# The last 2 KB of a load by another DMA queue, which leaves one DMA engine out

## The chip, the cores and the metric

The kernel runs on one core of a Trainium2 chip. The metric is device time in microseconds, from the start of the program on the chip to its end; the median of several runs counts. All engines of the core (TensorE, VectorE, ScalarE, GpSimd, SyncE) run programs of their own and meet through semaphores. Data moves between HBM and the on-chip memory (SBUF) by 16 DMA engines, which all queues share.

## The reference

```python
def setup_inputs():
    batch, heads, seq, dim = 8, 8, 512, 64
    return {"q": randn(batch, heads, seq, dim).astype(np.float32),
            "k": randn(batch, heads, seq, dim).astype(np.float32)}

def reference(q, k):
    scale = 1.0 / np.sqrt(q.shape[-1])
    return (np.einsum('bhqd,bhkd->bhqk', q, k) * scale).astype(np.float32)
```

For each of 64 pairs of batch and head, a 512 x 64 matrix of queries is multiplied with a 512 x 64 matrix of keys, and the 512 x 512 scores are scaled by 1/8. The inputs are 8.4 MB each, the output is 67.1 MB, all in float32.

## The kernel before

The batch is cut into four units (`UNITS`) of two batches each. A unit has four groups of work (two batches, and two halves of the heads), so there are 16 groups (`ALL`), of which each makes 2 x 8 matmuls and fills a quarter of the tile `big`. This tile holds 128 partitions x 4 parts x 32 KB. It is used twice: first the loads of unit `v` land in part `v` (`xf(v)`, 16 KB of k and 16 KB of q in each partition), later the scores are gathered there for the stores.

**Loads.** The first k load is cut in two halves, one issued by SyncE and one by ScalarE (line 72). The seven others are issued by SyncE in the order q0, k1, q1, k2, q2, k3, q3, each with a semaphore of its own (lines 81 to 84). A load fills 128 partitions with one contiguous run of 16 KB from HBM each, 2 MB in all. SyncE issues all of them without any wait, and the DMA engines work through them in that order.

**Casts.** GpSimd waits for each load and casts it to bfloat16 in two halves (lines 113 to 136), into a layout that lets VectorE turn pairs of values at once. There are slots for three units (`SLOTS`), so the casts of the last unit wait until VectorE has turned unit 0 (`turned`, line 115). The last two casts are those of q of the last unit; they wait for `load_sems[7]`.

**Turning.** VectorE turns keys and queries by 32 x 32 transposes (lines 191 to 238) into `kT` and `qz`.

**Matmuls and evacuation.** TensorE multiplies in a loop of four rounds of four groups (lines 141 to 164). ScalarE (and VectorE for six pieces) scales the sums from PSUM into `big` (lines 170 to 186), 2048 values per partition at a time.

**Stores.** SyncE stores `big` to HBM as soon as the groups are there (lines 93 to 107): two stores of 4 MB and seven of 8 MB. When a store has landed, its semaphore (`free0`, `free1`) lets TensorE begin the groups that will fill that part again, so two stores are under way in turn. At the end SyncE waits until the last two have landed (line 109). Loads and stores of SyncE share one DMA queue, so that on each DMA engine the stores stand behind the loads.

Of the kernel before, what the change touches and what calls it, by code (L numbers as in the profile page):

```python
# [5 lines left out]
def kernel(  # L6
# [5 lines left out]
    nc = tc.nc  # L12
    B, H, S, D = q.shape
    scale = 1.0 / (D ** 0.5)
    P = 128
    Q = 32
    UNITS = B // 2
# [4 lines left out]
    RO = 8  # L22
# [2 lines left out]
    ALL = 2 * B  # L25
    SETS = 2 * UNITS
    SLOTS = UNITS - 1

    f32 = mybir.dt.float32
    bf16 = mybir.dt.bfloat16  # L30
# [6 lines left out]
    sem = {name: nc.alloc_semaphore(name) for name in names}  # L37
    load_sems = [nc.alloc_semaphore(f"load{n}") for n in range(2 * UNITS)]
    halves = [load_sems[0], nc.alloc_semaphore("load0b")]

    q_r = q.rearrange("(v b) (x s h) (m j) d -> v (s h m) (b x) (j d)", b=2, x=2, s=2, j=R)
# [7 lines left out]
    bigs = [big[:, n] for n in range(UNITS)]  # L52
    xb = nc.alloc_sbuf_tensor("xb", [P, 2 * SLOTS, J, D, 2], bf16)[:]
    kT = nc.alloc_sbuf_tensor("kT", [P, 2 * G, S], bf16)[:]
# [2 lines left out]

    xw = xb.rearrange("p n w d e -> p n (w d e)").bitcast(f32).rearrange(
        "p n (w d) -> p n w d", d=D)
    kw = kT.bitcast(f32)  # L60
    qw = qz.bitcast(f32)

    def xf(v):
        return bigs[v].rearrange("p x i k -> p (x i k)").rearrange("p (x s c) -> p x s c", x=2, s=2)

    def slot(v, x):
        return v % SLOTS * 2 + x

    for s, queue in enumerate((nc.sync, nc.scalar)):
        first_load = queue.dma_start(
            out=xf(0)[:, 0, s].rearrange("p (x c) -> p x c", x=2), in_=k_0[s]
# [4 lines left out]

    for n in range(1, 2 * UNITS):
        v, x = divmod(n, 2)
        nc.sync.dma_start(out=xf(v)[:, x].rearrange("p s c -> p (s c)"), in_=(k_r, q_r)[x][v]
                          ).then_inc(load_sems[n], 16)

    def store(to, tiles):
# [22 lines left out]

    for v in range(UNITS):
        if v == SLOTS:
            nc.gpsimd.wait_ge(sem["turned"], 1)
            nc.gpsimd.sem_inc(sem["free1"], 1)
        for x in range(2):
            if v or x:
                nc.gpsimd.wait_ge(load_sems[2 * v + x], 16)
            for s in range(2):  # L120
                if v == x == 0:
                    nc.gpsimd.wait_ge(halves[s], 16)
                src = xf(v)[:, x, s]
                dst = xb[:, slot(v, x)]
                if x == 0:
                    src = src.rearrange("p (w e d) -> p w e d", e=2, d=D)
                    dst = dst[:, s * J // 2:(s + 1) * J // 2].rearrange("p w d e -> p w e d")
                else:
                    src = src.rearrange("p (jj e i d) -> p jj e i d", e=2, i=RO, d=D)
                    dst = dst.rearrange("p (i jj) d e -> p jj e i d", i=RO)[  # L130
                        :, s * JJ // 2:(s + 1) * JJ // 2]
                cast = nc.gpsimd.tensor_copy(out=dst, in_=src)  # L132
            cast.then_inc(sem["ready"], 1)
        if v % 2 == 0:
            nc.gpsimd.wait_ge(sem["ready"], 2 * v + 2)
            nc.gpsimd.sem_inc(sem[f"free{v // 2}"], 32)
# [132 lines left out]
```

## Time and profile before

| | |
|---|---|
| Time, median of 3 runs | 200.11 us (200.09 to 200.56) |
| Span of the profiled execution | 199.1 us |
| Moved by DMA | 83.90 MB, mean 421 GB/s |
| HBM read, written | 16.78 MB, 67.11 MB |
| Casts on GpSimd | 16, 2470 ns each |
| Evacuations on ScalarE | 58, 1888 ns each |
| Loads: issue to landing | 11.5 / 24.2 / 37.1 us (least, median, most) |
| First store issued, last store issued | 35.8 us, 175.9 us |

The page gives for each engine the time in which it was busy, its share of the span, and how many instructions it ran. One row shows the DMA engines in 40 slices of the span, as the mean busy share of all 16 in tenths, 9 for 90% or more. The DMA queues have rows of their own: packets, megabytes, and the time that the packets took as a share of 16 engines' span. A row of a timeline gives the start and the length of an instruction in us, its engine, line and tiles, and in brackets how long the engine had been idle and what ended that. For a queue (SPq) the length is that of the issuing, or from the first to the last of several. A row of waits gives the sum in us, the number of waits and the longest. Beside these views the trace holds a record for each DMA packet (start, length, queue, bytes; not the engine) and the time of each addition that a DMA engine makes to a semaphore.

### The profile page before, as it was taken

The page shows a single profiled execution, that of the slowest core. Times are in us where ns is not written, and L with a number is a line of the kernel's source. Part 1 is how long each engine was busy: PE and PEld are TensorE (multiplying, and loading weights), DVE is VectorE, ACT ScalarE, POOL GpSimd, SP SyncE. Part 2 cuts the span into 40 slices and gives each one's busy share as a digit, 9 for nine tenths or more (in the row PEclk, how much of TensorE's full clock was granted, in tenths as well). Part 3 has the DMA queues.
Part 4 walks back from the last instruction along what each step waited for, and adds up shares of the span by engine and source line. Part 5 has one row for each costly group of instructions (what it writes and reads, how often), then busy time and mean ns, then how long its engine had stood idle before and what let it go on. Part 6 is the DMA issues. An engine that isn't in the chain of part 4 may idle for free.

```text
span 199.1 us, 729 instructions
## 1 busy us (share of the span) xinstructions
PE 79.9 (40%) x256; PEld 23.5 (12%) x256; DVE 113.8 (57%) x61; ACT 105.6 (53%) x59; POOL 38.9 (20%) x20
## 2 busy tenths in 40 slices
PE   0000356546624662565257516550766076600000
PEld 0000011111101110111021102110211021100000
DVE  4238999999478039944993599369926500400000
ACT  2000049949970977197629752974397449730000
POOL 0399999699000000000000000000000000000000
PEclk9999999979995899589957975998599859995555
DMA  6999999999999999999999999999999999999995
GB/s 199 449 431 428 425 421 425 431 438 441 434 428 421 421 421 421 474 441 434 428 428 421 421 430 434 456 434 441 428 428 428 421 421 434 448 441 448 428 428 224
DMA packets 3746, 83.90 MB, mean 421 GB/s; under 512 B 288, under 2 KB 288, under 8 KB 800
## 3 DMA queue, kind: packets, MB, share of 16 engines
q1 hardware_dynamic: 3472, 82.84, 97.2%
q10 hardware_dynamic: 272, 1.05, 1.3%
q14 instruction: 2, 0.02, 0.0%
HBM read 16.78 MB, written 67.11 MB: 421 GB/s over the span
## 4 chain that ended last, share of the span: by engine, by line
DMA 41%; ACT 32%; PE 6%; DVE 4%; POOL 2%; issue 0%; SPq 0%
DMA out_dram<-big 35%; ACT big L179 32%; PE ps L158 6%; DMA big<-in_q_dram 6%; DVE qz L205 4%; POOL xb L132 2%; SPq L89 0%; SPq L107 0%
## 5 line engine op out<-in xcount | busy, mean ns | idle before, releaser
L179 ACT ACTIVATE big<-ps 128x2048 f32<-128x2048 f32 x58 | 104.3, 1888 | 68.3 <-PE ps L158 68.3
L158 PE MATMUL ps<-kT,qz 128*128 128x512 bf16 x256 | 79.9, 450 | 94.0 <-DMA out_dram<-big 35.8
L205 DVE STREAM_TRANSPOSE qz<-xb 32x1024 f32<-32x1024 f32 (+1 forms) x36 | 65.2, 1810 | 1.3 <-POOL xb L132 0.7
L158 PEld LDWEIGHTS ps<-kT,qz 128*128 128x128 bf16 x256 | 23.5, 110 | 149.8 <-ACT big L179 48.7
L132 POOL CAST xb<-big 128x2048 bf16<-128x2048 f32 x16 | 38.7, 2470 | 10.3 <-DMA big<-in_k_dram 7.8
L177 DVE TENSOR_SCALAR big<-ps 128x2048 f32<-128x2048 f32 x6 | 13.8, 2292 | 43.2 <-PE ps L158 43.2
L200 DVE STREAM_TRANSPOSE kT<-xb 64x1024 f32<-64x1024 f32 (+1 forms) x18 | 31.4, 1747 | 11.5 <-POOL xb L132 6.8
L212 DVE MEMSET qz<- 128x4096 uint32 x1 | 3.5, 3472 | 2.9 <-PEq L77 2.9
L179 ACT ACT_TABLE_LOAD x1 | 1.3, 1283 | 2.0 <-PEq L77 2.0
L253 POOL MEMSET const-float32-0.0<- 128x1 f32 x1 | 0.1, 98 | 0.2 <-issue 0.2
L253 POOL MEMSET const-bfloat16-1.0<- 128x1 bf16 x1 | 0.1, 101 | 0.0
L253 POOL MEMSET const-uint8-127<- 128x1 uint8 x1 | 0.1, 101 | 0.0
L253 POOL MEMSET const-float32-1.0<- 128x1 f32 x1 | 0.1, 98 | 0.0
## 6 DMA issues: line engine op xcount, KB each, us to landing
out_dram<-big SPq DMA_DIRECT2D x7, 8192.0 KB
big<-in_q_dram SPq DMA_DIRECT2D x4, 2048.0 KB, 24.2
out_dram<-big SPq DMA_DIRECT2D x2, 4096.0 KB
big<-in_k_dram SPq DMA_DIRECT2D x3, 2048.0 KB, 24.2
big<-in_k_dram ACTq DMA_DIRECT2D x1, 1024.0 KB, 9.0
big<-in_k_dram SPq DMA_DIRECT2D x1, 1024.0 KB, 7.5
```

Source lines behind the costliest of these rows:

```text
L132: cast = nc.gpsimd.tensor_copy(out=dst, in_=src)
L158: ins = pe.matmul(out=ps[:, i], lhsT=qz[:, 2 * t + x, i], rhs=kT[:, 2 * t + x], start=True, stop=True)
L177: freed = nc.vector.tensor_scalar_mul(out=to, in0=src, scalar1=scale)
L179: freed = nc.scalar.mul(out=to, in_=src, mul=scale)
L200: return nc.vector.transpose(out=out, in_=src)
L205: return nc.vector.transpose(out=qw[d:d + Q, b % 2 * G:(b % 2 + 1) * G, rows, h * Q:(h + 1) * Q].rearrange("d g i (m jj) -> d i jj m g", j ...
L212: nc.vector.memset(qz, 0.0).then_inc(sem["zeroed"], 1)
L253: nc = _bacc.Bacc("TRN2", target_bir_lowering=False, num_devices=1)
```

## The change

The last load, q of unit 3, is cut. Of the 16 KB in each partition the first 14 KB (`CUT` = 3584 values) come as before from SyncE, in one transfer of 128 partitions. The last 2 KB come in another way:

- for the first 120 partitions (`MOST`) by one transfer that GpSimd issues on its software queue, before its first cast;
- for the last 8 partitions by two transfers of 4 partitions each, which SyncE issues behind the large one.

Ahead of its transfer GpSimd resets the cursor of its queue and moves 5 x 2 runs of 32 bytes into a small tile `step` that nobody reads[...]. The purpose is that the 120 partitions go to 15 DMA engines, 8 each, without number 4, and the 8 others to the engines 0 to 3. Engine 4 so carries 16 KB less, and engines 0 to 3 carry 4 KB more each. The total of the bytes stays, but for the 320 bytes of `step`.

Before the last two casts GpSimd now waits for both of its transfers (`rest`, 32) and for the three of SyncE (48 on the last load's semaphore).

```diff
+    CUT = RO * S - 512
+    MOST = 120
...
+    rest_sem = nc.alloc_semaphore("rest")
...
+    step = nc.alloc_sbuf_tensor("step", [5, 2, 8], f32)[:]
...
-    for n in range(1, 2 * UNITS):
+    last_q = xf(UNITS - 1)[:, 1].rearrange("p s c -> p (s c)")
+    for n in range(1, 2 * UNITS - 1):
         v, x = divmod(n, 2)
         nc.sync.dma_start(out=xf(v)[:, x].rearrange("p s c -> p (s c)"), in_=(k_r, q_r)[x][v]
                           ).then_inc(load_sems[n], 16)
+    nc.sync.dma_start(out=last_q[:, :CUT], in_=q_r[UNITS - 1, :, :, :CUT]).then_inc(load_sems[-1], 16)
+    for n in range(MOST // 4, P // 4):
+        nc.sync.dma_start(out=last_q[4 * n:4 * n + 4, CUT:], in_=q_r[UNITS - 1, n, :, CUT:]
+                          ).then_inc(load_sems[-1], 16)
...
+    nc.gpsimd.inc_swdge_sem([], [], mode="reset_dge_cursor")
+    nc.gpsimd.dma_start(out=step, in_=q_r[0, 0:5, 0:2, 0:8]).then_inc(rest_sem, 16)
+    nc.gpsimd.dma_start(out=last_q[:MOST, CUT:], in_=q_r[UNITS - 1, :MOST // 4, :, CUT:]
+                        ).then_inc(rest_sem, 16)
...
-            if v or x:
+            if 2 * v + x == 2 * UNITS - 1:
+                nc.gpsimd.wait_ge(rest_sem, 32)
+                nc.gpsimd.wait_ge(load_sems[-1], 48)
+            elif v or x:
                 nc.gpsimd.wait_ge(load_sems[2 * v + x], 16)
```

## The prediction

> **What bounds the kernel now.** I read the page from its DMA rows down, because a kernel that moves 83.9 MB in 199 us is suspect there first.
>
> ```profile
> span 199.1 us, 729 instructions
> PE 79.9 (40%) x256; PEld 23.5 (12%) x256; DVE 113.8 (57%) x61; ACT 105.6 (53%) x59; POOL 38.9 (20%) x20
> DMA  6999999999999999999999999999999999999995
> q1 hardware_dynamic: 3472, 82.84, 97.2%
> q10 hardware_dynamic: 272, 1.05, 1.3%
> q14 instruction: 2, 0.02, 0.0%
> ```
>
> No compute engine passes 57%, while the 16 DMA engines are at 90% or more in every slice but the first and the last. Queue 1 alone takes 97.2% of sixteen engines' span. So the time is the bytes of the busiest DMA engine over its rate. The chain of waits shows "DMA out_dram<-big" pieces of 23.4 us; they are pieces of a queue that never runs empty, as the sync queue's timeline and its waits show:
>
> ```profile
> 5.96 0.62 SPq L83 DMA_DIRECT2D big<-in_q_dram  x1
> 35.77 23.55 SPq L89 DMA_DIRECT2D out_dram<-big  x3
> 97.73 0.61 SPq L89 DMA_DIRECT2D out_dram<-big  x1
> 175.90 0.61 SPq L89 DMA_DIRECT2D out_dram<-big  x1
> ...
> SPq L109 <- DMA out_dram<-big: 22.6, 1, 22.6
> ```
>
> All loads are issued by 6.6 us and land by 43.08 us, the first store stands ready from 35.77 us, and the last, issued at 175.90, lands 23 us later although its 8 MB take only about 19.4 us: it queues. In the packet records nearly every 32 KB store packet takes 1213 to 1214 ns, one per 1210.5 ns on an engine. That is 27 GB/s each, without a gap.
>
> The tail is the point here. The page's last DMA digit, 5, covers 5 us, and the windows view shows in which part of it traffic is thin:
>
> ```profile
> 197.00:199.12 2.12, 0.00 (x0) 0.00 (x0) 0.00 (x0) 0.00 (x0) 0.00 (x0) 0.50 0.04 15
> ```
>
> Packets count where they start, so hardly anything starts after 197.00. Each DMA engine adds one to a store's semaphore when its share has landed. Those times, from the trace, in us:
>
> ```
> store   1st     8th     15th    last    last - 8th
>  1    52.18   52.30   52.65   52.82   0.52
>  3    81.26   81.37   81.86   82.01   0.63
>  5   119.99  120.14  120.81  121.09   0.95
>  7   158.75  158.98  159.53  160.17   1.19
>  9   197.52  197.75  198.25  199.07   1.33
> ```
>
> The last arrival falls behind steadily, and at the end it is 0.83 us behind the fifteenth. The packet records show why: among the store packets is a row of packets of 1220 to 1236 ns that follow each other at 1221 to 1224 ns. That is one engine, about 11 ns slower per packet; times 128 packets this is 1.4 us. One slow engine therefore sets the end, and the other fifteen wait up to 1.5 us for it. The trace doesn't record its number.
>
> [...]
>
> **The change part by part.** First, cost per row. A 4 KB row follows the next at 155.5 ns and a 16 KB row at 607.5 ns, so one KB costs 37.7 ns and each row about 5 ns besides.
>
> Engine 4 has 8 rows of the last q load. They shrink by 2 KB each: 8 x 2 x 37.7 = 0.60 us saved. A second reading agrees: load landings lie 4.89 us apart for 128 KB per engine, so 16 KB are 0.61 us. It gains two 32-byte rows of the step transfer (8-byte to 32-byte packets of the instruction queue took 7 ns) and at most two semaphore posts (9 ns): 0.03 to 0.05 us. Net 0.56 us less on engine 4.
>
> Engines 5 to 15 move the same bytes in 8 rows more: 8 x 5 ns, and posts: 0.06 to 0.07 us more. Engines 0 to 3 get two rows of 2 KB (80 ns each) on top and two posts: 0.25 us more in all.
>
> If engine 4 is the slow one, its end moves from 199.07 to 198.51 us. The fifteenth, at 198.25, moves to 198.32, or to 198.50 if it is one of 0 to 3. Either way the new end is about 198.51, 0.56 us sooner. The whole kernel is nowhere else shortened.
>
> What lies beside other work: SyncE issues two instructions more (0.6 us each, from 6.6 to 7.8 us), ahead of a store that isn't ready before 35.77. The waits added at the last q cast (rest and 48 of the load) stand on GpSimd. Queued behind them are only the two last casts, and VectorE's turning of the last q behind those. The trace puts them late enough:
>
> ```profile
> 8.28 4.81 POOL L132 CAST xb<-big 128x2048 bf16<-128x2048 f32 x2 [7.83 <-DMA big<-in_k_dram]
> 39.81 9.67 POOL L132 CAST xb<-big 128x2048 bf16<-128x2048 f32 x4 [1.87 <-DVE qz L205]
> ...
> 2.89 3.47 DVE L212 MEMSET qz<- 128x4096 uint32 x1 [2.89 <-PEq L77]
> ```
>
> The last q casts begin at about 44.6 us, and the load landed at 43.08. So these waits cost nothing.
>
> GpSimd's two transfers stand ahead of the first cast. GpSimd idles until 8.28 us, so up to about 6 us of issuing are free. No row of before prices such an issue. From below: 0.6 us each, as on sync. [...]
>
> Their 16 KB per engine also come ahead of the first loads and delay them by 0.6 us. This moves the first casts from 8.28 to about 8.9, and through casts, transposes and evacuations the third store from 58.65 to about 59.3. That store is needed when the first two have drained, at 61.9 on the first engines, less 1.1 us from issue to first packet: slack is 61.9 - 1.1 - 58.65 = 2.1 us. Of that 0.6 is used. No bubble, no cost.
>
> Sum: 200.11 - 0.56 = 199.55 us.
>
> **The rivals.** First, slower: the late engine isn't number 4. Then its work grows by 0.07 us, or 0.25 us on engines 0 to 3: 200.18 to 200.36 us. For it speaks that the trace gives no number; against it, nothing in the profile. Second, slower by more: GpSimd's descriptors come so late that the slack of 2.1 us is spent. With a first cast 3 to 4 us late [...] and the 0.6 us for bytes, 1.5 to 2.5 us of empty queue appear on all engines: 200.11 + 1.5 to 2.5 - 0.56, so 201.05 to 202.05 us. Against it: GpSimd has nothing else to do before 8.28 us. Third, a smaller gain: rows written by the software queue cost more than 5 ns, say 60, so that fifteen engines lose 0.5 us, and another becomes the last, at 198.75 or 198.9: 199.8 to 199.95 us. For it: before has no queue of this kind; against it: 4 KB rows in two alternating queues cost no extra time.
>
> **How the numbers follow.** Forecast 0.58; late engine another one 0.13; large slowdown 0.16; other engines become last 0.13. The forecast's own spread is 0.2 us around 199.55, since the drift of 1.4 us need not be the same in each run; it lies almost on the bound of 0.3% (199.51), so I give six tenths of it, 0.36, to faster (the reading by landings, 0.61, passes the bound), and the rest, with the third rival and most of the first, to no change: faster 0.36, same 0.45, slower 0.19. From 199.35 to 200.40 the range holds the forecast, the first and the third rival, leaving out the large slowdown and a little on the fast side.
>
> **What would show it.** A software queue with some 120 packets of 2 KB on the page; the last landing of the ninth store within 0.3 us of the fifteenth instead of 0.83; its end near 198.5. If the gap stays at 0.8 or grows, the wrong engine was relieved. If a zero or a low DMA digit appears near 60 us, or the first cast starts after 10.5 us, the second rival is right. If the fifteenth moved by 0.5 us, the third. The forecast is wrong altogether if the slow engine is slow only while it is being recorded, for then timed runs have nothing to relieve.

## The result, and the profile after

The changed kernel is slower: 200.87 us (median of 8 runs, 200.41 to 201.20) against 200.11, a ratio of 1.0032 with a 95% interval of 1.0020 to 1.0045. The prediction was 199.55, range 199.35 to 200.40.

The page of the changed kernel, its span, two rows of slices and its DMA queues:

```profile
span 199.5 us, 731 instructions
...
DMA  6999999999999999999999999999999999999997
GB/s 205 389 395 427 424 427 443 415 449 427 420 453 466 420 440 420 420 420 420 427 427 466 460 422 420 420 416 427 434 420 434 447 440 440 427 427 427 420 427 309
...
q1 hardware_dynamic: 3488, 82.59, 97.2%
q10 hardware_dynamic: 272, 1.05, 1.4%
q0 software_dynamic: 112, 0.25, 0.4%
```

Read the two rows together. The engines are as busy as before from the second slice on, and the last digit went from 5 to 7: the tail is fuller, as it was meant to be. But the second and third slice move 389 and 395 GB/s. The same row of the kernel before, which the prediction didn't show:

```profile
GB/s 199 449 431 428 425 421 425 431 438 441 434 428 421 421 421 421 474 441 434 428 428 421 421 430 434 456 434 441 428 428 428 421 421 434 448 441 448 428 428 224
```

So the DMA engines are busy and slow, early on. The windows view (columns: us, busy time and instructions of PE, PEld, DVE, ACT, POOL, clock, DMA share, GB/s) narrows it to a stretch of 4.3 us, first the kernel before, then after:

```profile
8.00:12.30 4.30, 0.00 (x0) 0.00 (x0) 0.00 (x0) 0.00 (x0) 4.02 (x2) 1.00 1.00 430
```

```profile
8.00:12.30 4.30, 0.00 (x0) 0.00 (x0) 0.00 (x0) 0.00 (x0) 3.65 (x2) 1.00 1.03 347
```

430 minus 347 GB/s for 4.3 us is 0.36 MB, or 0.83 us at 430 GB/s. The packet records say what is slow: in this stretch a 16 KB packet of queue 1 takes 800 ns (median of 75) where it took 611. This holds not only on engines that serve the software queue. The first q load lands on its sixteen engines at 14.16 and then from 14.48 to 15.09 us, against 12.79 to 13.43 before. The engine at 14.16, alone in front, is the one left out: its row of packets (how rows are followed is told below) has none of the software queue's 60 packets of 4 KB. It still lands 0.73 us later than the last of all engines did before, and its 16 KB packets in this stretch take 792, 806, 802 and 748 ns.

The timeline of GpSimd shows the issue to be cheap and early, and the first q cast late:

```profile
2.67 0.69 POOL L124 DMA_DIRECT2D step<-in_q_dram  x1 [2.22 <-POOLq L82]
3.35 0.61 POOL L125 DMA_DIRECT2D big<-in_q_dram  x1
8.65 4.81 POOL L152 CAST xb<-big 128x2048 bf16<-128x2048 f32 x2 [4.69 <-DMA big<-in_k_dram]
15.14 4.84 POOL L152 CAST xb<-big 128x2048 bf16<-128x2048 f32 x2 [1.68 <-DMA big<-in_q_dram]
```

Before, those two casts began at 8.28 and 13.49 us. Where the time goes is best seen in the landings, in us. "Mean" is over sixteen engines; the last column is how far the last engine of the ninth store lies behind that mean. For the last q load the table has the mean end of each engine's last packet instead, because in the changed kernel 24 additions to the semaphore belong to this load, not 16.

```
          last k load  last q load  store 1   store 9                   last
          mean         mean end     mean      mean    15th     last     - mean
before    37.50        42.33        52.39     197.87  198.25   199.07   1.21
after     39.07        42.93        53.11     198.93  199.26   199.46   0.53
```

The last k load should come 0.6 us later, since 16 KB per engine were put ahead of it; it comes 1.57 later, so 0.97 us are lost. The last q load should come no later, since the bytes are the same; it comes 0.60 later, and the first store 0.72. Part of the 0.97 us is hidden there because the kernel before loses time of its own at this point: from the last packet of its last k load to that of its last q load pass 5.31 us, where its loads otherwise land 4.89 apart. At the end the last engine is 0.67 us less late and the mean is 1.06 us later: together 0.39, which is the difference of the two spans (199.5 and 199.1).

The engine that ends last is no longer the slow one. The packet records don't name the engine, but in the stores each packet starts within 8 ns of the end of another, or some 300 ns after it, so that sixteen rows of packets can be followed. In the changed kernel the slow row (1221 ns from packet to packet on the mean) is the one that leads at the first store, and its last packet ends at 198.77 us. It is the row without 4 KB packets of the software queue; four others have two packets of 2 KB each. Two other rows end later, at 198.85 and 199.05. On each of them one packet of the instruction queue (8 KB, 309 ns, at 130.62 and at 117.25 us) goes between the stores, and the store packet behind it takes 1333 and 1572 ns.

The recorded execution of the kernel before took 200.45 us, longer than its median; that of after took 200.86. So the recorded pair shows 0.41 us and the medians 0.76; the mechanism is measured below on a pair whose recorded times agree with their medians (k16_step and k15_later).

### The profile page after: what moved, and what is told of

Its sections match the earlier page's. It is cut to its first block, busy times and chain, and to the rows that moved or that the text cites. A ratio compares the mean times of both kernels' runs of the same rounds, so it can differ in the third digit from the quotient of the medians.

```text
span 199.5 us, 731 instructions
## 1 busy us (share of the span) xinstructions
PE 81.7 (41%) x252; PEld 23.7 (12%) x256; DVE 113.8 (57%) x61; ACT 105.8 (53%) x59; POOL 40.2 (20%) x22
## 4 chain that ended last, share of the span: by engine, by line
DMA 41%; ACT 32%; PE 7%; DVE 4%; POOL 2%; issue 0%; SPq 0%
DMA out_dram<-big 35%; ACT big L199 32%; PE ps L178 7%; DMA big<-in_q_dram 7%; DVE qz L225 4%; POOL xb L152 2%; SPq L99 0%; SPq L117 0%
## 5 line engine op out<-in xcount | busy, mean ns | idle before, releaser
L178 PE MATMUL ps<-kT,qz 128*128 128x512 bf16 x252 | 81.7, 462 | 92.7 <-DMA out_dram<-big 34.3
L124 POOL DMA_DIRECT2D step<-in_q_dram x1 | 0.7, 688 | 2.2 <-POOLq L82 2.2
L125 POOL DMA_DIRECT2D big<-in_q_dram x1 | 0.6, 607 | 0.0
```

The costliest lines, as they stand in the source:

```text
L124: nc.gpsimd.dma_start(out=step, in_=q_r[0, 0:5, 0:2, 0:8]).then_inc(rest_sem, 16)
L125: nc.gpsimd.dma_start(out=last_q[:MOST, CUT:], in_=q_r[UNITS - 1, :MOST // 4, :, CUT:]).then_inc(rest_sem, 16)
L178: ins = pe.matmul(out=ps[:, i], lhsT=qz[:, 2 * t + x, i], rhs=kT[:, 2 * t + x], start=True, stop=True)
```

## The experiments

Theories that came and went: the shape of the rows (2 KB runs, 32 KB apart in HBM), the software queue as such, VectorE's memset, the first microseconds of the kernel, the step transfer, engines that write into partitions which others fill in the full-width loads, and fewer than sixteen engines. A ratio is against runs of the kernel before on the same chip, taken beside those of the experiment; three chips took part. Of each edit only the lines that matter are shown; sizes of tiles and counts of waits that follow from them are left out. Rates without a view are those of the packet records, each packet spread over its length, in slices of 0.5 us.

**The rows' shape.** act_rows moves the same rows of all 128 partitions by ScalarE's hardware queue on sixteen engines.

```diff
+    nc.scalar.dma_start(out=last_q[:, CUT:], in_=q_r[UNITS - 1, :, :, CUT:]).then_inc(rest_sem, 16)
...
+    nc.sync.dma_start(out=last_q[:, :CUT], in_=q_r[UNITS - 1, :, :, :CUT]).then_inc(load_sems[-1], 16)
```

> Part of the change alone: the last q load is cut at the same place, but its last 2 KB come for all 128 partitions by ScalarE's hardware queue (8 rows on each of 16 engines), early, with no software queue and no engine left out. In the changed kernel the DMA rate fell from 430 to about 330 GB/s between 8 and 12.3 us, on every engine. Theory R (the rows themselves, 2 KB pieces that lie 16 KB or more apart in HBM, slow all engines): the same fall, 16 KB packets of 800 ns instead of 611 ns, q0 landing after 14.4 us instead of 13.43, and with no relief of the late engine about 201.1 us. Theory S (the software queue, its descriptors or its way of being served, slows them): rate stays at 420 to 430 GB/s, q0 landing 0.6 us later than before (about 14.0), and 200.1 to 200.3 us.

200.19 us against 200.16 (ratio 1.0001, 0.9992 to 1.0010). While these rows alternate with 16 KB packets (10 to 15 us) the rate stays at 422 to 429 GB/s, and a 16 KB packet takes 611 ns. The rows' shape costs nothing.

**The software transfer with contiguous rows.** sw_contig leaves the last q load whole and adds, as extra work, 120 contiguous rows of 2 KB by the software queue into a spare tile.

```diff
+    flat = q.rearrange("b h (m e) d -> (b h m) (e d)", e=8)
+    nc.gpsimd.inc_swdge_sem([], [], mode="reset_dge_cursor")
+    nc.gpsimd.dma_start(out=step, in_=q_r[0, 0:5, 0:2, 0:8]).then_inc(rest_sem, 16)
+    nc.gpsimd.dma_start(out=spare[:120], in_=flat[:120]).then_inc(rest_sem, 16)
```

> The kernel before with the software transfers added as they are in the change [...], but the rows are contiguous in HBM (2 KB apart) and go into a tile that nobody reads; all loads stay whole, so 15 engines carry 16 KB more than before and engine 4 does not. Theory S: the rate falls to about 330 GB/s while that queue is served; all engines lose 1 us, so about 201.1 us or more. Theory R: 16 KB packets stay at 611 ns; 15 engines lose only 0.6 us for the bytes, the late one nothing, so the last landing stays near 199.1 and the time at 200.1 to 200.3 us.

201.71 us, ratio 1.0080 (1.0060 to 1.0101). The rate falls to 331 to 364 GB/s in the same stretch and the 16 KB packets take 752 ns. With act_rows, this pointed to the software queue itself. That was too early a conclusion, as will be seen. One thing is not as it was meant: the engine left out isn't number 4. The row of packets that leads in the stores needs 8.47 us for seven packets, as ordinary engines do; the slow one (8.57) stands in the middle. In memset_later below, on the same chip and with the same step, the slow row leads. Why another engine is left out here isn't shown.

**Another engine left out.** left_out_8 is the changed kernel with a step of nine rows.

```diff
-    step = nc.alloc_sbuf_tensor("step", [5, 2, 8], f32)[:]
+    step = nc.alloc_sbuf_tensor("step", [9, 2, 8], f32)[:]
...
-    nc.gpsimd.dma_start(out=step, in_=q_r[0, 0:5, 0:2, 0:8]).then_inc(rest_sem, 16)
+    nc.gpsimd.dma_start(out=step, in_=q_r[0, 0:9, 0:2, 0:8]).then_inc(rest_sem, 16)
```

> The changed kernel [...]. Theory that engine 4 is the late one and was relieved: the last landing of the ninth store is again 0.7 to 0.8 us behind the fifteenth (0.2 in the changed kernel), and the time rises by about 0.5 us to 201.3 us. Rival (the gap closed because all engines were delayed or by chance): landings as in the changed kernel, 200.9 us.

201.13 us (200.91 to 201.20), ratio 1.0044 (1.0029 to 1.0058): above the changed kernel by 0.26 us, which speaks for number 4, but the two were not run side by side and their intervals overlap. The last engine was only 0.12 us behind the fifteenth (199.74 and 199.61), not 0.7. A miss in that detail, and too small a difference to decide on; the comparison is repeated below.

**The memset.** memset_later lets VectorE's memset wait for the software queue.

```diff
+    nc.vector.wait_ge(rest_sem, 32)
     nc.vector.memset(qz, 0.0).then_inc(sem["zeroed"], 1)
```

> The changed kernel with VectorE's zeroing of the query tile behind the landing of the software transfers. In the changed kernel GpSimd's instructions end by 4 us but the first software packet starts at 6.5 us, 0.13 us after the zeroing ends. Theory that the zeroing holds back the descriptors: the first packet starts near 4 us, before any 16 KB packet runs, and the rows end by about 8 us. Then, if the loss comes only where those rows run beside 16 KB packets, the q0 landing comes back to about 14.0 us and the time falls to 200.0 to 200.3 us; if the rows cost the same wherever they run, the time stays at 200.9 us. Rival (descriptors merely take 3 us to act): first packet still at 6.5 us and no change.

The first software packet came at 6.60 us instead of 6.5, and the slow stretch stayed. The memset didn't hold the descriptors back. The kernel took 202.18 us (ratio 1.0107, 1.0091 to 1.0124) for a reason of its own, which the timeline of VectorE shows:

```profile
13.68 3.47 DVE L233 MEMSET qz<- 128x4096 uint32 x1 [13.68 <-POOL xb L152]
```

The transposes behind it started 3.6 us later than in the changed kernel, and the third store was issued at 61.97 us, 3.3 us later than in the kernel before. The first engine was through with the second store at 62.38, sooner than the 1.1 us from issue to first packet allow: the queue ran dry. The slack that the prediction counted on, 2.1 us, is about as small as it said.

**Sixteen engines by the software queue.** sw_rows_16 moves the rows of all 128 partitions so, at the same place, with no step and no small transfers.

```diff
-    MOST = 120
+    MOST = 128
...
-    nc.gpsimd.dma_start(out=step, in_=q_r[0, 0:5, 0:2, 0:8]).then_inc(rest_sem, 16)
```

> The software queue alone, without the relief: the last 2 KB of the last q load come for all 128 partitions by GpSimd's queue on all 16 engines; no step transfer, no small transfers on engines 0 to 3. No engine carries more or less than before. Theory that the change is a cost of about 1.1 us for serving the software queue less about 0.6 us of relief, plus slower packets where one store follows another: 201.1 to 201.7 us, and the last landing of the ninth store again 0.5 to 0.8 us behind the fifteenth on a chip where one engine is slower. Rival (the small transfers on four engines and the exclusion do the harm): 200.2 us.

200.42 us, ratio 1.0014 (1.0007 to 1.0020): 0.27 us lost, a fifth of what was expected. Low rates (295 to 374 GB/s) are found only from 6.5 to 8.5 us, where the loads of unit 0 still run on two hardware queues. The forecast had taken the software queue itself for the cause of the whole loss. It isn't.

**Half of the rows.** half sends 60 rows by the software queue, on 15 engines.

```diff
-    MOST = 120
+    MOST = 60
...
+    n = MOST // 4
+    nc.sync.dma_start(out=last_q[MOST:P // 2, CUT:], in_=q_r[UNITS - 1, n, :, CUT:]).then_inc(load_sems[-1], 16)
+    nc.sync.dma_start(out=last_q[P // 2:, CUT:], in_=q_r[UNITS - 1, n + 1:, :, CUT:]).then_inc(load_sems[-1], 16)
```

> The changed kernel with half of its rows on the software queue: 60 partitions (4 rows for each of 15 engines, engine 4 left out), the 2 KB of 64 others by SyncE's queue on 16 engines, of 4 by the same on engines 0 to 3. Relief of engine 4 is 8 KB, 0.3 us. Theory that the loss lasts as long as rows of the software queue are served: the stretch of slow 16 KB packets is about half as long (2 us instead of 4), 0.5 us lost, time near 200.3 to 200.5 us. Rival (a fixed price of using that queue at all): 1 us lost as before with half the relief, 201.1 us or more.

200.71 us, ratio 1.0025 (1.0014 to 1.0036), above the 200.3 to 200.5 expected. The slow stretch lasts from 8.0 to 10.3 us, half as long, with 16 KB packets at 764 ns. So the stretch goes with the number of rows that the 15 engines move. The relief of 0.3 us, which was to make the rest of the gain, didn't show here (last minus fifteenth 0.55 us).

**Relief without a second queue.** hw_prefix takes 768 bytes from each row and moves them by eight transfers of SyncE on four engines, at the end of the loads.

```diff
+    CUT = RO * S - 192
...
+    for n in range(8):
+        to = last_q[16 * n:16 * n + 16, CUT:]
+        nc.sync.dma_start(out=to, in_=q_r[UNITS - 1, 4 * n:4 * n + 4, :, CUT:]).then_inc(load_sems[-1], 16)
```

> Relief without the software queue: the last 768 bytes of each row of the last q load come by SyncE in eight transfers of 16 partitions, each on engines 0 to 3. Engines 4 to 15 carry 6 KB less than before, 0.23 us; engines 0 to 3 carry 18 KB in 32 short rows more, 0.84 us, for which they have about 1.3 us of room behind the slow one. Theory that one engine among 4 to 15 sets the end: 0.2 us sooner, 199.9 us. Rival (the slow engine is one of 0 to 3, or it changes from run to run or chip to chip): 0.8 us later, 200.9 us, or a mixture.

201.18 us, ratio 1.0054 (1.0041 to 1.0068). Four engines land the first store at 53.67 to 53.82 us, the others from 51.82 to 52.28: these four carry too much, and the kernel is 1.0 us slower. This is no way to the relief.

**Which engine is slow.** marked adds work to the kernel before so that engines can be told apart: four extra transfers on ScalarE's hardware queue with 121, 119, 85 and 68 rows.

```diff
+    for n, rows in enumerate((121, 119, 85, 68)):
+        nc.scalar.dma_start(out=spare[:rows, n], in_=flat[n * P:n * P + rows, :480]).then_inc(mark_sem, 16)
```

> The kernel before with marks by which its packets tell the engine's number: ScalarE's queue moves rows of 1920 bytes into a tile that nobody reads, 11 each on engines 0 to 10, 17 each on 0 to 6, on 0 to 4 and on 0 to 3 (79 ns a row). Landings of the first store should then fall in groups, each behind the one before: 11 to 15, 7 to 10 (0.9 us later), 5 and 6 (1.3 us more), 4 (1.3 more), 0 to 3 (1.3 more). The time is that of the latest group, some 5 us later than before. Theory that the slow engine is number 4 always: the packets of 1221 to 1224 ns step belong to the single engine of the fourth group. Rival (another engine on another chip): to another group.

The first store lands in groups: five engines at 54.82 to 55.00 us, four at 55.54 to 56.04, two at 57.52 and 57.53, one at 58.45, four at 59.52 to 59.55. These are the sizes that come out if the four transfers ran on 11, 7, 5 and 4 engines, the fewer always among the more. No view gives an engine's number; counted from the group with the most marks (0 to 3), the one by itself is number 4, and that is all that a number stands for here. It needs 9.751 us from there to the next store's landing, where the others need 9.65: 12.6 ns more for each of eight packets. So on this chip the slow engine is number 4, wherever it stands in the order. The same landings show something else: the five engines in front carry none of the marks, and still land the first store at least 2.0 us later than any engine of the kernel before (52.18 to 52.82 us). 16 KB packets beside the marks take 669 ns here. (The extra work makes the kernel 209.56 us long, in a single run, so its time says nothing.)

**Issue ahead of the barrier.** early puts GpSimd's two transfers before the close of the tile context.

```diff
+    nc.gpsimd.inc_swdge_sem([], [], mode="reset_dge_cursor")
+    for rest in (nc.gpsimd.dma_start(out=step, in_=q_r[0, 0:5, 0:2, 0:8]),
+                 nc.gpsimd.dma_start(out=last_q[:MOST, CUT:], in_=q_r[UNITS - 1, :MOST // 4, :, CUT:])):
+        rest.then_inc(rest_sem, 16)
+        tc.no_tile_sem_insts.add(rest.ins.name)
     tc.close()
```

> The changed kernel with GpSimd's two transfers issued ahead of the barrier at the program's start (at about 0.5 us instead of 2.7), so that their rows run beside the 4 KB rows of the first k load and are done before the 16 KB packets begin at 7.3 us. Theory that the loss grows with the time for which rows of the software queue stand beside packets of 16 KB (4.3 us in the changed kernel, 2 us and little loss with 16 engines, which began earlier): loss 0.2 to 0.3 us, relief 0.55 us, 199.8 to 199.9 us, faster than the kernel before. Rival (a transfer on 15 engines costs 1 us wherever it runs): 200.9 us as the changed kernel.

204.93 us, ratio 1.0238. The timeline of SyncE:

```profile
0.74 0.46 SPq L83 DMA_DIRECT2D big<-in_k_dram  x1
10.47 0.63 SPq L94 DMA_DIRECT2D big<-in_q_dram  x1
```

Its second load is issued at 10.47 us, 0.7 us after the last software row had landed (9.77), and the DMA engines stood empty from 9.4 to 11.5 us; in the kernel before it is issued at 1.96. ScalarE and GpSimd, too, go on only at 10.47 us. That the barrier waits for GpSimd's transfers fits, and is argued from these times alone; on the question here the run says nothing.

**No step.** k15_first is the changed kernel without the step transfer; fifteen engines take the rows, and the one left out was meant to be another than number 4.

```diff
-    nc.gpsimd.dma_start(out=step, in_=q_r[0, 0:5, 0:2, 0:8]).then_inc(rest_sem, 16)
```

> The changed kernel without the step transfer: 120 rows on 15 engines [...]. Theory of time (the step transfer makes the rows come 0.6 us later and so run beside 16 KB packets): first 4 KB packets of the software queue at 6.5 us, stretch of low rate over by about 9 us, time near 200.5 us. Rival (15 engines or rows in that form are slow as such): stretch of 4 us again and 201.2 us or more.

200.75 us, ratio 1.0033 (1.0022 to 1.0043); 16 KB packets beside the rows at 802 ns (median of 24). The time lies between the two expectations, so it settled little at that place.

**Later.** sw16_later is sw_rows_16 with the transfer behind GpSimd's casts of unit 0, at 18.9 us.

```diff
     for v in range(UNITS):
+        if v == 1:
+            nc.gpsimd.inc_swdge_sem([], [], mode="reset_dge_cursor")
+            nc.gpsimd.dma_start(out=last_q[:MOST, CUT:], in_=q_r[UNITS - 1, :MOST // 4, :, CUT:]
+                                ).then_inc(rest_sem, 16)
```

> The kernel with all 128 rows on the software queue and 16 engines, issued behind the casts of unit 0 (at about 19 us instead of 2.5), where only 16 KB packets run beside them. Theory of time: 16 KB packets of about 800 ns for some 4 us, about 1 us lost on all engines, 201.2 us against 200.42 for the same transfer issued early. Rival (16 engines serve the queue cheaply in any company): 200.4 us.

200.07 us against 200.08, ratio 1.0002 (0.9993 to 1.0010), below both expectations. The software queue's packets (two rows, 4 KB, 159 ns each) alternate with 16 KB packets of 624 ns, and nothing is lost. That left two readings: the first microseconds, or fifteen engines. k15_later is the changed kernel with its two transfers at this later place, and k15_later_8 the same with a step of nine rows.

```diff
+        if v == 1:
+            nc.gpsimd.inc_swdge_sem([], [], mode="reset_dge_cursor")
+            nc.gpsimd.dma_start(out=step, in_=q_r[0, 0:5, 0:2, 0:8]).then_inc(rest_sem, 16)
+            nc.gpsimd.dma_start(out=last_q[:MOST, CUT:], in_=q_r[UNITS - 1, :MOST // 4, :, CUT:]
+                                ).then_inc(rest_sem, 16)
```

> The changed kernel with its two software-queue transfers (the step of 5 rows and the 120 rows of 2 KB on 15 engines without number 4) issued behind GpSimd's casts of unit 0, at about 19 us, instead of at 2.7 us; nothing is left out. Form theory (a software transfer on 15 engines slows all queues while its packets are in flight, whenever that is): from about 23 us on a stretch of 2.5 to 4 us at 300 to 350 GB/s in place of 430, hardware packets of 16 KB at 700 to 900 ns in place of 611, 0.6 to 1.0 us lost, of which the relief gives back 0.56: 200.1 to 200.9 us. Start theory (the loss needs the first microseconds, where the loads of unit 0 on two hardware queues still run): no such stretch, packets stay at 611 ns, and the prediction's relief comes through whole: 199.4 to 199.7 us, with the last landing of the last store 0.2 us behind the 15th in place of 0.8.

> The same with a step of 9 rows[...]; nothing is left out of the computation. If number 4 is the slow engine and the relief is worth 0.56 us: this kernel lies 0.5 to 0.7 us above the one that leaves out number 4, at 200.0 to 200.2 us where the start theory holds and at 200.6 to 201.5 us where the form theory holds; the last landing of the last store stays 0.6 to 0.9 us behind the 15th. If any engine would do (the relief is only fewer bytes in small rows): equal to the other within 0.15 us.

200.70 us (1.0035, 1.0021 to 1.0049) and 201.17 (1.0053, 1.0040 to 1.0067). The slow stretch moved with the transfer. Number 4 left out is 0.47 us faster than another engine left out; the last engine is 0.08 us behind the fifteenth in the one and 0.43 in the other. The packets show that the two steps left out different engines: the row that leads in the stores takes 8.59 us for seven packets in k15_later, as the slow engine does, and 8.47 in k15_later_8, as an ordinary one. They also show the engine left out to be slowed like the others: in k15_later one row has no packet of the software queue, and its 16 KB packets in the slow stretch take 827, 889, 835, 767 and 766 ns.

**What of the fifteen engines.** k16_step adds the step to sw16_later. k15_own is k15_later without the step: the rows of partitions 0 to 119 on fifteen engines. I assumed, without a trace for it, that each engine so takes 8 partitions in a row, and the same 8 as in the full-width loads. k15_off takes partitions 8 to 127 instead, so that by the same assumption each of them writes into its neighbour's. own_sides was to keep number 4's relief with hardly an engine off the partitions that this assumption gives it: 88 rows on eleven engines by the software queue, and by SyncE on four engines the 32 rows of partitions 0 to 31 and the 8 of partitions 32 to 39. The line that k16_step adds:

```diff
+            nc.gpsimd.dma_start(out=step, in_=q_r[0, 0:5, 0:2, 0:8]).then_inc(rest_sem, 16)
```

From k15_own to k15_off:

```diff
-            nc.gpsimd.dma_start(out=last_q[:MOST, CUT:], in_=q_r[UNITS - 1, :MOST // 4, :, CUT:]
+            nc.gpsimd.dma_start(out=last_q[LEAST:, CUT:], in_=q_r[UNITS - 1, LEAST // 4:, :, CUT:]
```

In own_sides, beside that last line with LEAST = 40:

```diff
+    for j in range(8):
+        nc.sync.dma_start(out=last_q[j:LEAST - 8:8, CUT:], in_=q_r[UNITS - 1, j // 4:LEAST // 4 - 2:2, j % 4, CUT:]
+                          ).then_inc(load_sems[-1], 16)
```

> sw16_later (all 128 rows of 2 KB by the software queue on 16 engines, behind the casts of unit 0, 200.07 us) with the step of 5 rows ahead of it; nothing is left out. [...] If the step's small transfer is what slows the queues: a stretch at 300 to 350 GB/s from 23 us on and 200.5 to 200.9 us. If the 15 engines or the foreign partitions do it: the rate stays at 425 to 432 GB/s and the time at 200.0 to 200.2 us.

> k15_later (200.70 us) without the step: 120 rows [...], at 19 us; nothing is left out of the computation. [...] Foreign-partition theory: no slow stretch, 427 to 432 GB/s, 16 KB packets at 611 ns, 200.0 to 200.2 us. Form theory (15 engines as such): the stretch of 4 us at 300 to 350 GB/s stays, 200.7 to 201.1 us.

> k15_own with the 120 rows taken from partitions 8 to 127 in place of 0 to 119, the first 8 by engines 0 to 3: no step[...]; nothing is left out. Foreign-partition theory: the slow stretch is there, 3 to 5 us at 290 to 350 GB/s, and the time is 0.5 to 1.0 us above that of k15_own, at 200.6 to 201.2 us. Form theory: the same time as k15_own within 0.15 us. Step theory: no slow stretch in either.

> k15_later's relief of number 4 [...]: 88 rows of partitions 40 to 127 on engines 5 to 15 by the software queue (the step of 5 rows ahead of it), rows of partitions 0 to 31 by eight transfers of four rows, 8 partitions apart, on engines 0 to 3, the 8 rows of partitions 32 to 39 on engines 0 to 3 as in the changed kernel; nothing is left out. Foreign-partition theory: no slow stretch beyond 1 us, number 4's relief of 0.5 us (as k15_later stood to k15_later_8) comes through: 199.45 to 199.75 us, ahead of both kernels. Form theory (a software transfer on fewer than 16 engines): stretch of 3 us or more, 200.3 to 200.8 us.

Times: k16_step 200.10 us (1.0001, 0.9992 to 1.0009), k15_own 200.81 (1.0028, 1.0017 to 1.0039), k15_off 200.85 (1.0038, 1.0025 to 1.0052), own_sides 200.84 (1.0035, 1.0021 to 1.0049). The windows view from 22.5 to 28.5 us, of k16_step and of k15_own:

```profile
22.50:28.50 6.00, 3.38 (x8) 1.01 (x9) 5.92 (x5) 1.88 (x1) 6.00 (x4) 1.00 1.00 415
```

```profile
22.50:28.50 6.00, 3.20 (x8) 0.92 (x9) 5.90 (x6) 1.88 (x1) 6.00 (x3) 1.00 1.01 363
```

The last number is what counts: 415 GB/s with sixteen engines and the step, 363 with fifteen and no step; the kernel before makes 434 there. The step is cleared by k16_step's time and by this line. With eleven engines (own_sides) the kernel is as slow as with fifteen, against the 199.45 to 199.75 us hoped for. And k15_own and k15_off agree within 0.04 us, so a shift of the 15-engine transfer by 8 partitions changed nothing.

That does not clear the theory of foreign partitions. These runs test it only if the assumption about the 8 partitions holds, and no view here shows which partitions an engine writes.

**A hardware queue on fifteen engines.** The missing corner: act_k15 is act_rows with 120 of its rows on fifteen engines, again without any software queue.

```diff
-    nc.scalar.dma_start(out=last_q[:, CUT:], in_=q_r[UNITS - 1, :, :, CUT:]).then_inc(rest_sem, 16)
+    nc.scalar.dma_start(out=last_q[:MOST, CUT:], in_=q_r[UNITS - 1, :MOST // 4, :, CUT:]).then_inc(rest_sem, 16)
```

> act_rows (the 2 KB rows of all 128 partitions by ScalarE's hardware queue on 16 engines, 200.19 us) with 120 of the rows on engines 0 to 14 by ScalarE's hardware queue and the last 8 by engines 0 to 3 as in the changed kernel; no software queue, nothing left out. If a second queue that serves only 15 of the engines slows all of them, whichever queue it is: a stretch of 2 to 4 us at 300 to 360 GB/s after the first loads, packets of 16 KB at 700 to 900 ns, 200.6 to 201.1 us. If it takes a software-queue transfer on fewer than 16 engines: the rate stays at 425 to 432 GB/s, packets at 611 ns, 200.1 to 200.5 us (engines 0 to 3 carry 4 KB more each, engine 15 16 KB less).

200.81 us, ratio 1.0034 (1.0023 to 1.0044). The windows view, of act_rows and then of act_k15:

```profile
8.00:10.00 2.00, 0.00 (x0) 0.00 (x0) 0.00 (x0) 0.00 (x0) 1.94 (x1) 1.00 1.05 446
10.00:14.00 4.00, 0.00 (x0) 0.00 (x0) 0.98 (x1) 0.00 (x0) 2.98 (x3) 1.00 1.05 442
```

```profile
8.00:10.00 2.00, 0.00 (x0) 0.00 (x0) 0.00 (x0) 0.00 (x0) 1.99 (x1) 1.00 1.05 441
10.00:14.00 4.00, 0.00 (x0) 0.00 (x0) 1.07 (x1) 0.00 (x0) 2.82 (x2) 1.00 1.00 378
```

From 8 to 10 us both are largely still at the small loads of unit 0, and equal. From 10 to 14, where the 2 KB rows run beside the q load, fifteen engines make 378 GB/s where sixteen make 442 (the view counts a packet where it starts). The row without small packets has 16 KB packets of 656 to 695 ns here. So it doesn't take the software queue: a second transfer on fewer than sixteen engines does it, on either kind of queue.

All runs in which the small rows stood beside the large loads, but for marked, in one table. The third column is the median of a 16 KB packet of queue 1 while the small rows run beside it; the fourth is the mean landing of the last k load. By its bytes the latter should be 37.50 us plus up to 0.6, so 38.1 (half: 37.8).

```
             second transfer               16 KB packet   last k load   kernel
before       none                          611 ns         37.50 us      200.11 us
act_rows     ScalarE, 16 engines           611            38.28         200.19
sw16_later   GpSimd, 16, later             624            38.27         200.07
k16_step     GpSimd, 16, step, later       621            38.12         200.10
sw_rows_16   GpSimd, 16                    611            38.31         200.42
act_k15      ScalarE, 15 engines           685            38.61         200.81
left_out_8   GpSimd, 15, step of 9         748            39.05         201.13
sw_contig    GpSimd, 15, extra rows        752            38.89         201.71
own_sides    GpSimd, 11, step, later       753            38.74         200.84
half         GpSimd, 15, half the rows     764            38.32         200.71
k15_own      GpSimd, 15, later             786            39.05         200.81
k15_later_8  GpSimd, 15, step of 9, later  791            39.20         201.17
after        GpSimd, 15, step              800            39.07         200.87
k15_first    GpSimd, 15                    802            38.75         200.75
memset_later GpSimd, 15, step              804            39.12         202.18
k15_later    GpSimd, 15, step, later       814            39.17         200.70
k15_off      GpSimd, 15, later, shifted    814            39.05         200.85
```

With sixteen engines the last k load keeps to its bytes within 0.2 us; with fewer it loses 0.5 to 1.1.

## Why the prediction was wrong

**The step that failed** is the cost of the rows: "Engines 5 to 15 move the same bytes in 8 rows more: 8 x 5 ns, and posts: 0.06 to 0.07 us more." That priced a row by what it adds on its own engine. The rows do cost little there (159 to 200 ns for a packet of two rows, where 4 KB rows of the kernel before take 159). What they cost is paid by the other queue: a 16 KB packet takes 800 ns in place of 611 for as long as the 15-engine transfer lasts, on the engine left out too. By the prediction's terms the sixteen engines together should have been later by under 0.1 us on the mean. The first store measured 0.72 us (mean landing, 53.11 against 52.39), and the clean pair below 0.90. And "the whole kernel is nowhere else shortened" had no counterpart that asked whether it is lengthened elsewhere.

**The rivals.** The third, "rows written by the software queue cost more than 5 ns, say 60", had the right neighbourhood, but let fifteen engines lose 0.5 us and number 4 keep its gain. Its counter-argument, that alternating queues cost nothing in the trace of before, was true only of transfers of sixteen engines each: act_rows and sw16_later confirm it there. The second rival (descriptors too late) was wrong: the first software packet came at 6.5 us, there was no bubble near 60 us, and the first cast began at 8.65. VectorE's memset, which ends at 6.38 in the changed kernel, did not hold that packet back: with the memset out of the way it came at 6.60. The 3.8 us from the start of GpSimd's first instruction (2.67) to its first packet have a cause that isn't shown: issued at 18.94 us, with no memset near, the first packet came at 22.88. The first rival (not number 4) was wrong too. The result lies between the ranges of the first and the second rival, and none of the three foresaw it.

**What was right.** The late engine is number 4: marked shows it. The prediction had no reason for this number, and its trace shows none, so that much was luck. The bytes moved between the engines as the change meant: in its trace one row has none of the 60 packets of 4 KB and it is the slow one, and four rows have two packets of 2 KB each. A step of nine rows left out another engine (8.47 us for the leading row of k15_later_8, 8.59 in k15_later); sw_contig, with a step of five, doesn't fit, for there the engine left out (8.47) isn't the slow one (8.57). The relief came. In the five recorded runs in which number 4 was relieved of the whole 16 KB (after, memset_later, early, k15_later, own_sides) the last engine of the last store lies 0.49 to 0.91 us behind the mean of the sixteen; in the twelve that leave out none, or another (shown by the leading rows in sw_contig and k15_later_8, elsewhere only meant), it is 0.83 to 1.28 (half, hw_prefix and marked, where the bytes of the engines differ otherwise, aren't counted). The averages are 0.68 and 1.11, so the end gains 0.43 us where 0.56 was foretold; the timed pair k15_later and k15_later_8 gives 0.47. It was predicted that last and fifteenth would lie within 0.3 us; they lie 0.20 apart. But this sign was a poor one: in left_out_8, without the relief, they lie 0.12 apart. Every run has one store packet of 1565 to 1641 ns, so that a second engine is late beside number 4. In the changed kernel the two engines that the instruction queue held up set the end, and more relief of number 4 would have gained nothing there. The page also has 60 software packets of 4 KB, two rows each, where 120 of 2 KB were expected. Issue on SyncE and GpSimd, the waits at the last casts, and the slack of the third store cost nothing, as said.

**The sum.** k15_later against k16_step is the clean pair: the same place, the same step, 120 rows instead of 128. The mean of the last store moves from 197.73 to 198.63 us (+0.90), the last engine's lag from 1.00 to 0.70 (-0.30), together +0.60; the spans differ by 0.6 and the medians by 0.60. Loss and relief are both there, and the loss is larger. As far as one run with half of the rows shows, it shrinks with the rows moved while the relief does too, so less of the change didn't turn the balance.

**What stays open.** Why a transfer on fewer than sixteen engines slows the packets of all sixteen isn't shown. A reason would have to fit three things. The engine left out is slowed too (766 to 889 ns in k15_later), though it carries none of the second transfer's rows. Either kind of queue does it (685 ns in act_k15, 748 to 814 with the software queue), and the stretch grows with the number of rows (2.3 us with 60 in half, 4.3 with 120 in the changed kernel). And the lengthening is close to the length of the small packet beside it (190 ns with 4 KB packets of 159 to 200, 74 with 2 KB packets of 84), as if each large packet once waited for a small one; that is a guess from these lengths. To tell the partitions from the number of engines, 64 rows would have to go on the same eight engines once into one set of partitions and once into another; that wasn't tried.

Two smaller things have no cause either. sw_rows_16 loses 0.27 us with sixteen engines, at the place where the software queue meets two hardware queues. And in after, left_out_8, memset_later, hw_prefix and marked 41 to 77 of the 2048 store packets take 1265 to 1295 ns in place of 1214, in all other runs at most 9; from the first store to the ninth the mean landing of after takes 0.3 us longer than that of the kernel before (145.81 against 145.48 us), and that of k15_later no longer (145.41). No kernel run here was faster than the kernel before; act_rows, sw16_later and k16_step equal it, with nothing relieved.

## What to carry to other kernels

When a transfer is moved to a second queue, cost it in the packets of the first queue too: compare the length of one kind of packet with and without company, not only the bytes. Here a second transfer on fewer than sixteen engines lengthened the first queue's packets by 12 to 33% while it lasted, on the engine left out too, and one on all sixteen cost nothing beside the large loads (611 to 624 ns, 200.07 to 200.19 us), whichever queue carried it. Ask of a transfer with another shape not only how many bytes each engine gets, but also on how many of the engines it runs beside the large ones.

## What the runs showed of the hardware that was not expected

- A transfer on 15 or 11 DMA engines beside a 16-engine one lengthens the latter's 16 KB packets from 611 ns to 685 (hardware queue, 2 KB packets) or 748 to 814 (software queue, 4 KB packets), on the engine left out too (766 to 889 in k15_later). On 16 engines they stay at 611 to 624. Whether the number of engines or the partitions that they write makes the difference isn't shown.
- One DMA engine takes 11 to 13 ns more per 32 KB store packet than the others (9.751 against 9.65 us for eight), which makes it about 1 us late after nine stores. On the chip where it was identified (marked) it is the one by itself in the landings, number 4 in their order.
- A packet of the instruction queue (8 KB, 309 ns) at about 117 us and one at about 130 us each hold up the stores of one DMA engine: in after the next store packet starts 302 ns late and takes 1572 and 1333 ns in place of 1214.
- From the start of GpSimd's DMA instruction to its first packet pass 3.8 to 4.0 us (2.67 to 6.52 in after, 18.94 to 22.88 in sw16_later), with or without a memset on VectorE.
- With GpSimd's transfers issued ahead of the closing barrier of the tile context, SyncE, ScalarE and GpSimd went on only at 10.47 us; that the barrier waited for these transfers is argued.
